# Split weights at rotating columns: nine weight buffers made 64 bytes longer, each block begun 0 to 15 columns in

## The chip, the cores and the metric

The kernel runs on one core of a Trainium2 chip. The metric is the device time of one execution in microseconds; it is compared with the time of the kernel before on the same chip.

## The reference

Two transformer-like blocks follow each other on 512 tokens of width 1024, all in fp32. Most of the work is in products of activations with weights:

```python
def squared_relu_mlp(h, w1, w2):
    return jnp.square(jax.nn.relu(h @ w1)) @ w2
...
    for i in range(DEPTH):
...
        x = x + rms_norm(m, g[1])
        h = rms_norm(x, g[2])
        x = x + rms_norm(squared_relu_mlp(h, mlp_w1[i], mlp_w2[i]), g[3])
...
    ffn = (jax.nn.silu(n2 @ w_gate) * (n2 @ w_up)) @ w_down
    return h + ffn
```

`DEPTH` is 2: in the first of its rounds `m` comes from a short convolution beside a latent attention, in the second from a convolution of 31 taps between two products. The last lines are of the second block, which has attention with a forget gate and 16 extra tokens, and pooling, ahead of them. The MLP width is 4096 in the first block, 2816 in the second.

## The kernel before

Activations lie transposed: channels in the 128 partitions, the 512 tokens along the free dimension. So an activation tile is 128 x 512, and a product is a sum over tiles of 128 channels, accumulated in one PSUM buffer `ps`.

Precision comes from splitting. Each fp32 number is kept as a high part, rounded to the format fp32r by a copy, and a low part, the difference. A tile of activations `P` is `[128, 2, 512]`: high parts in the first 512 columns, low parts in the next. Weights are split in the same way into buffers `W`, `[128, 2, 512]`. `mm3` then makes three matmuls for each product (lines 357 to 359): high weights by high activations, high weights by low activations, low weights by high activations. The weights are the stationary operand (128 columns, loaded by a weight load of their own ahead of every matmul), the activations are the moving one, 512 columns at a time or 256 where a stage works in halves.

All weights stand in one array in the order in which they are used. `make_plan` writes that order down as pieces of 128 columns (some have 256, those of the forget gate 8), and `pack` puts pieces into blocks of up to 512 columns, and two blocks into one load. There are 578 blocks. The class `Weights` runs through them: `dma` brings a load of two blocks into one of three `raw` buffers on SyncE's queue, and `advance` splits a block into one of nine `W` buffers: the high part on ScalarE (line 284), the low part on VectorE (line 286), or on GpSimd for 55 blocks of the convolution module. In the program's order a block is split four blocks before it is used (`AHEAD`); in time ScalarE runs ahead as far as the nine buffers allow. A call of `W(name, k, t)` gives the high and the low columns of a piece: columns `c` to `c + n` of its block.

In the built program every `W` buffer has 4096 bytes in each partition and so has every `P` buffer; the first `W` buffer begins 163,072 bytes behind the first `P` buffer, which is 637 times 256.

Four other places matter below:

- `run_pe` (line 1112) makes part of the 31-tap convolution with matmuls: the stationary operand is a tap matrix of `W`, the moving one 256 columns of a tile `x` that begin at column `s`, 0 to 15 in turn. High parts of `x` lie in columns 0 to 271, low parts in 272 to 543. It makes 384 matmuls.
- `forget_gate` (line 1333) uses eight pieces of 8 columns, by 512 moving columns. They stand in one block behind three pieces of 128 columns, at columns 384, 392 and so on to 440. Each is used for three matmuls.
- `conv_dve` (line 1068) makes the other half of the convolution on VectorE: tap `t` reads 512 columns of a tile from column `t` on, 0 to 30 (line 1082). The tile is written from column 15 on (line 1139).
- `conv_pe` (line 1099) writes its tile `x` on ScalarE from columns 8 and 7 on (line 1109).

Of the kernel before, what the change touches and what calls it, by code (L numbers as in the profile page):

```python
# [12 lines left out]
F32R = mybir.dt.float32r  # L13
# [8 lines left out]
T = 512  # L22
# [222 lines left out]
class Weights:  # L245
# [30 lines left out]
    def advance(self, b):  # L276
        nc = self.nc
        while self.nsplit <= min(b + self.AHEAD, len(self.blocks) - 1):
            load, start, cols = self.blocks[self.nsplit]
            while self.ndma <= min(load + self.RAW - 1, len(self.loads) - 1):  # L280
                self.dma()
            w = self.w_pool.tile([128, 2, T], F32R, name="W")
            r = self.raw[load][:, start:start + cols]
            nc.scalar.activation(out=w[:, 0, :cols], in_=r, func=AF.Copy)  # L284
            eng = nc.gpsimd if self.nsplit in self.on_pool else nc.vector
            eng.tensor_sub(out=w[:, 1, :cols], in0=r, in1=w[:, 0, :cols].bitcast(F32))  # L286
            self.w[self.nsplit] = w
            self.nsplit += 1
# [1452 lines left out]
```

## Time and profile before

| | |
|---|---|
| median of 2 runs | 1764.86 us (1763.05 to 1766.67) |
| profiled execution | 1765.45 us |
| its span, first to last instruction | 1763.7 us |
| TensorE busy | 1723.2 us, 98% |
| VectorE busy | 1091.3 us, 62% |
| ScalarE busy | 802.3 us, 45% |
| GpSimd busy | 272.2 us, 15% |
| matmuls | 8828 |
| DMA | 167.26 MB, mean 95 GB/s |

The times of instructions come from one profiled execution. PE is TensorE's matmul, PEld its weight load, which overlaps matmuls, DVE is VectorE, ACT is ScalarE, POOL is GpSimd. A matmul's shown duration reaches from its start to a modelled end and is longer than the distance to the next start, so distances are read from starts.

### The profile page before, as it was taken

What the parts mean: (1) busy time and instruction counts of PE and PEld (TensorE: products, weight loads), DVE (VectorE), ACT (ScalarE), POOL (GpSimd) and SP (SyncE); (2) the same over time, 40 slices, a digit from 0 to 9 for tenths busy, and PEclk for the clock granted to TensorE, in tenths of its full rate; (3) what the DMA queues carried; (4) which work ended last, traced back from release to release, by engine and by line L of the source; (5) the groups of instructions that cost most, each with busy time, mean ns of one, the idle gap of its engine ahead of it and who ended that gap; (6) DMA issues with size and microseconds to landing.
All of it is one profiled execution on the core that took longest, in us unless ns stands there. A gap on an engine that the chain in (4) does not pass through costs nothing.

```text
span 1763.7 us, 23141 instructions
## 1 busy us (share of the span) xinstructions
PE 1723.2 (98%) x8828; PEld 1459.7 (83%) x8828; DVE 1091.3 (62%) x1771; ACT 802.3 (45%) x1461; POOL 272.2 (15%) x339
## 2 busy tenths in 40 slices
PE   9999999999999999999999999989999999999999
PEld 7778888888888878999888888888687888888887
DVE  6988786344444789958544444487897555344452
ACT  6546655333333445675543333357665443232331
POOL 3413330000000355503000000041223200000000
PEclk9999999999999999999999999999999999999999
DMA  5231313223322132512322222222223323222221
GB/s 196 73 106 55 108 49 120 96 98 101 100 96 96 49 108 96 180 60 73 118 99 96 96 96 96 96 96 69 78 62 98 98 98 101 97 96 96 96 96 60
DMA packets 49887, 167.26 MB, mean 95 GB/s; under 512 B 6848, under 2 KB 7296, under 8 KB 49776
## 3 DMA queue, kind: packets, MB, share of 16 engines
q1 hardware_dynamic: 47776, 160.70, 27.8%
q0 software_dynamic: 1936, 5.07, 1.0%
q8 instruction: 69, 1.13, 0.3%
q14 instruction: 42, 0.34, 0.1%
q10 hardware_dynamic: 64, 0.02, 0.0%
HBM read 158.25 MB, written 4.19 MB: 92 GB/s over the span
## 4 chain that ended last, share of the span: by engine, by line
PE 80%; DVE 11%; issue 3%; ACT 2%; POOL 2%; DMA 1%; SPq 0%; POOLq 0%; DVEq 0%; ACTq 0%
PE ps L358 26%; PE ps L357 26%; PE ps L359 26%; DVE P L968 1%; DVE W L286 1%; PE ps L623 1%; DVE P L401 1%; POOL P L971 1%; DVE S L1477 1%; DVE S L424 1%; DVE P L398 1%; DMA raw<-in_w 1%; ACT S L450 1%; DVE S L422 1%; DVE S L420 0%
## 5 line engine op out<-in xcount | busy, mean ns | idle before, releaser
L357 PE MATMUL ps<-P,W 128*128 128x512 f32 (+1 forms) x2541 | 928.2, 365 | 5.9 <-DVE S L1130 2.8
L358 PE MATMUL ps<-P,W 128*128 128x512 f32 (+1 forms) x2541 | 924.8, 364 | 5.8 <-DVE P L401 5.8
L359 PE MATMUL ps<-P,W 128*128 128x512 f32 (+1 forms) x2541 | 923.4, 364 | 0.0
L284 ACT ACTIVATE W<-raw 128x512 fp32r<-128x512 f32 x578 | 357.1, 629 | 651.4 <-PE ps L359 609.0
L286 DVE TENSOR_TENSOR W<-raw,W 128x512 fp32r<-128x512 f32 x523 | 371.4, 717 | 382.2 <-ACT W L284 379.6
L357 PEld LDWEIGHTS ps<-P,W 128*128 128x128 f32 x2541 | 482.2, 190 | 83.3 <-DVE S L1130 3.2
L358 PEld LDWEIGHTS ps<-P,W 128*128 128x128 f32 x2541 | 482.9, 190 | 81.0 <-DVE P L401 6.9
L359 PEld LDWEIGHTS ps<-P,W 128*128 128x128 f32 x2541 | 482.3, 190 | 75.3 <-DVE W L286 0.4
L971 POOL TENSOR_TENSOR P<-P 128x256 f32<-128x256 f32 x48 | 45.5, 956 | 773.3 <-DVE P L968 772.2
L398 DVE TENSOR_TENSOR P<-S,P 128x512 fp32r<-128x512 f32 (+3 forms) x134 | 93.8, 706 | 50.4 <-ACT P L397 49.8
L397 ACT ACTIVATE P<-S 128x512 fp32r<-128x512 f32 (+3 forms) x134 | 81.5, 614 | 63.8 <-DVE S L1664 25.9
L286 POOL TENSOR_TENSOR W<-raw,W 128x512 fp32r<-128x512 f32 x55 | 73.0, 1352 | 37.7 <-ACT W L284 33.7
L1082 DVE SCALAR_TENSOR_TENSOR ps<-P,vec,ps 128x512 f32<-128x512 f32 x116 | 77.8, 745 | 0.0
L400 ACT ACTIVATE P<-P,vec 128x256 fp32r<-128x256 f32 (+1 forms) x80 | 43.7, 549 | 50.4 <-POOL P L971 30.1
L1029 DVE SCALAR_TENSOR_TENSOR S<-ps,S 128x512 f32<-128x512 f32 x64 | 43.6, 689 | 34.1 <-PE ps L359 34.1
L401 DVE SCALAR_TENSOR_TENSOR P<-P,vec 128x256 fp32r<-128x256 f32 (+1 forms) x80 | 54.2, 691 | 9.7 <-ACT P L400 9.5
L470 POOL TENSOR_TENSOR S<-S 128x256 f32<-128x256 f32 (+1 forms) x45 | 48.1, 1069 | 76.6 <-ACT S L469 74.3
L469 ACT ACTIVATE S<-P 128x256 f32<-128x256 f32 (+1 forms) x105 | 46.4, 473 | 17.8 <-DVE P L1056 11.9
L636 POOL TENSOR_TENSOR P<-S,P 128x512 fp32r<-128x512 f32 (+1 forms) x24 | 34.3, 1428 | 112.3 <-DVE P L635 95.7
L1049 DVE TENSOR_TENSOR P<-ps,P 128x512 f32<-128x512 f32 x42 | 29.0, 691 | 28.7 <-PE ps L359 28.7
L623 PE MATMUL ps<-P 128*128 128x512 f32 (+3 forms) x160 | 41.2, 375 | 2.2 <-DVE S L1443 0.9
L470 DVE TENSOR_TENSOR S<-S 128x256 f32<-128x256 f32 (+1 forms) x60 | 33.1, 551 | 14.4 <-ACT S L469 13.4
(263 smaller groups left out, 1300.7 us busy)
## 6 DMA issues: line engine op xcount, KB each, us to landing
raw<-in_w SPq DMA_DIRECT2D x286, 512.0 KB
P<-in_xT SPq DMA_DIRECT2D x8, 256.0 KB
P<-in_xT POOLq DMA_DIRECT2D x8, 256.0 KB, 5.4
keep<-P SPq DMA_DIRECT2D x8, 256.0 KB
P<-P SPq DMA_DIRECT2D x16, 128.0 KB
P<-keep POOLq DMA_DIRECT2D x8, 256.0 KB, 5.4
out<-P SPq DMA_DIRECT2D x7, 256.0 KB
raw<-in_w SPq DMA_DIRECT2D x2, 256.0 KB
```

The source lines that it names most:

```text
L284: nc.scalar.activation(out=w[:, 0, :cols], in_=r, func=AF.Copy)
L286: eng.tensor_sub(out=w[:, 1, :cols], in0=r, in1=w[:, 0, :cols].bitcast(F32))
L357: mm(ps, w[0], x[0], start=first, stop=False)
L358: mm(ps, w[0], x[1], start=False, stop=False)
L359: mm(ps, w[1], x[0], start=False, stop=last)
L397: nc.scalar.activation(out=hi, in_=src, func=AF.Copy)
L398: nc.vector.tensor_sub(out=lo, in0=src, in1=hi.bitcast(F32))
L401: nc.vector.scalar_tensor_tensor(out=lo, in0=src, scalar=scale, in1=hi.bitcast(F32), op0=OP.mult, op1=OP.subtract)
L470: (eng or nc.vector).tensor_add(out=acc, in0=acc, in1=t)
L623: mm(o[:m], k, q[:, pl, c0:], start=n == 0 and m == 128, stop=n == len(keys) - 1 and mask is None)
L971: ins = eng.tensor_add(out=x[k][:, cols], in0=x[k][:, cols], in1=m[k][:, cols]).ins
L1082: V.scalar_tensor_tensor(out=dst if dst is not None and t == taps[-1] else acc, in0=u, scalar=w, in1=acc, op0=OP.mult, op1=OP.add)
```

## The change

Each `W` buffer gets 16 columns more (64 bytes in each partition). Block number `n` uses the 1024 columns that begin at column `n % 16` of its buffer, and views them as `[128, 2, 512]` again, so all reads and writes of the block go through the shifted view. `raw`, `P` and all other buffers stay where they are.

```diff
-            w = self.w_pool.tile([128, 2, T], F32R, name="W")
+
+            o = self.nsplit % 16
+            w = self.w_pool.tile([128, 2 * T + 16], F32R, name="W")[:, o:o + 2 * T].rearrange("p (l t) -> p l t", l=2)
             r = self.raw[load][:, start:start + cols]
             nc.scalar.activation(out=w[:, 0, :cols], in_=r, func=AF.Copy)
             eng = nc.gpsimd if self.nsplit in self.on_pool else nc.vector
```

The sequence of instructions on each engine, and what each waits for, is the same in both programs.

## Rows read from the trace of the kernel before

**Rows 1.** the page's first part: busy time of each engine

```profile
span 1763.7 us, 23141 instructions
...
PE 1723.2 (98%) x8828; PEld 1459.7 (83%) x8828; DVE 1091.3 (62%) x1771; ACT 802.3 (45%) x1461; POOL 272.2 (15%) x339
```

**Rows 2.** windows: busy by engine (instructions), granted clock, DMA share, GB/s

```profile
1000.00:1100.00 100.00, 100.00 (x443) 82.83 (x442) 45.57 (x66) 34.94 (x57) 0.00 (x0) 1.00 0.31 100
...
1200.00:1300.00 100.00, 94.26 (x639) 76.22 (x636) 88.77 (x186) 65.78 (x143) 17.66 (x17) 1.00 0.20 57
...
641.50:644.50 3.00, 3.00 (x8) 2.32 (x7) 3.00 (x6) 1.58 (x3) 0.01 (x1) 0.50 0.42 158
```

**Rows 3.** waits: engine, line <- releaser: us in total, times, longest

```profile
ACT W L284 <- PE ps L359: 609.0, 344, 2.9
...
DVE W L286 <- ACT W L284: 379.6, 304, 3.8
...
PEld ps L357 <- ACT W L284: 0.8, 1, 0.8
...
PEld ps L359 <- DVE W L286: 0.4, 1, 0.4
```

**Rows 4.** groups by shape, whole span: count, busy us, mean ns, idle before

```profile
L357 PE MATMUL ps<-P,W 128*128 128x512 f32 x1879 | 735.0, 391 | 4.0 <-DVE S L1130 2.8 <-ACT P L400 1.2
...
L357 PE MATMUL ps<-P,W 128*128 128x256 f32 x654 | 190.0, 291 | 1.9 <-ACT P L397 0.8 <-ACT P L400 0.6 <-DVE P L1689 0.5
...
L357 PEld LDWEIGHTS ps<-P,W 128*128 128x128 f32 x2533 | 481.5, 190 | 82.2 <-DVE S L1130 3.2 <-ACT P L400 2.4 <-ACT P L397 1.4
...
L284 ACT ACTIVATE W<-raw 128x512 fp32r<-128x512 f32 x576 | 356.2, 629 | 651.4 <-PE ps L359 609.0 <-DMA raw<-in_w 22.8 <-PE ps L1264 5.4
...
L286 DVE TENSOR_TENSOR W<-raw,W 128x512 fp32r<-128x512 f32 x521 | 370.3, 718 | 382.2 <-ACT W L284 379.6
```

**Rows 5.** timeline of TensorE at half clock: start us, us, instruction

```profile
641.95 0.63 PE L358 MATMUL ps<-P,W 128*128 128x512 f32 x1
...
644.08 0.63 PE L357 MATMUL ps<-P,W 128*128 128x512 f32 x1
```

**Rows 6.** timeline of TensorE, forget gate

```profile
1196.86 0.39 PE L357 MATMUL ps<-P,W 128*8 128x512 f32 x1
...
1197.54 0.40 PE L357 MATMUL ps<-P,W 128*8 128x512 f32 x1
...
1202.39 0.18 PE L357 MATMUL ps<-hm,W 128*8 128x32 f32 x1
```

**Rows 7.** timeline of TensorE, convolution's first matmul and the one after its last

```profile
696.10 0.28 PE L357 MATMUL ps<-P,W 128*128 128x256 f32 x1
...
741.38 0.38 PE L1177 MATMUL ps<-P,onesf 128*128 128x256 f32 x1
```

**Rows 8.** groups of TensorE in that convolution (one of three equal ones)

```profile
L358 PE MATMUL ps<-P,W 128*128 128x256 f32 x128 | 35.9, 280 | 0.0
```

**Rows 9.** timeline of TensorE, a run of 256-column matmuls after it

```profile
765.45 0.28 PE L357 MATMUL ps<-P,W 128*128 128x256 f32 x1
...
781.29 0.40 PE L357 MATMUL ps<-P,W 128*128 128x512 f32 x1
```

**Rows 10.** groups of TensorE in that run (one of three equal ones)

```profile
L358 PE MATMUL ps<-P,W 128*128 128x256 f32 x44 | 12.5, 283 | 0.0
```

**Rows 11.** weight loads of 64 and 32 columns: ns min/median/max

```profile
L1264 PEld LDWEIGHTS ps<-W,hm x80: 133/134/223, 1181.9 to 1331.8; 128*64 128x64 f32 x80
...
L1263 PEld LDWEIGHTS ps<-W,hm x70: 107/108/113, 1184.7 to 1331.7; 128*32 128x32 f32 x70
```

**Rows 12.** single lines with shifted columns: ns min/median/max

```profile
L1082 DVE SCALAR_TENSOR_TENSOR ps<-P,vec,ps x116: 736/744/753, 647.1 to 738.2; 128x512 f32<-128x512 f32 x116
...
L1109 ACT ACTIVATE P<-P x16: 657/661/682, 673.3 to 705.7; 64x512 fp32r<-64x512 f32 x16
...
L1139 DVE SCALAR_TENSOR_TENSOR P<-S,vec x4: 734/882/1292, 641.0 to 660.1; 128x512 f32<-128x512 f32 x4
```

## The prediction

> **What bounds the kernel now.** I read the page's busy times first, then equal stretches of the span, then who waits for whom, then the groups of instructions by shape, and last the starts of single matmuls. TensorE is busy 1723.2 of 1763.7 us [rows 1]. In a plain stretch of the MLP, 1000 to 1100 us, it is busy for all 100 us, while VectorE is busy 45.57 and ScalarE 34.94 [rows 2]. The waits say the same from the other side: the ScalarE half of the weight split stands 609.0 us waiting for a matmul to free a W buffer, and the VectorE half 379.6 us for the ScalarE half, but weight loads of lines 357 and 359 waited for a split only 0.8 and 0.4 us in the whole run [rows 3]. So the split runs ahead as far as nine buffers let it, and what sets the end is how long one matmul takes after another.
>
> I call that distance from start to start the pitch. TensorE's matmuls by weights of W are 3 x 1879 with 512 moving columns and 3 x 654 with 256, 7599 in all [rows 4]. [...] At the full clock one takes 226.7 ns ((1197.54 - 1196.86) / 3 in [rows 6]). [...]
>
> **What the change takes away, adds and moves.** No instruction is added, removed or put elsewhere on any engine, and no wait is: the sequence of all five engines is the one of before. Only addresses change. W buffers step by 4160 bytes instead of 4096, and a block begins 0 to 60 bytes behind its buffer's start. Today the stationary columns of a full block, and the moving columns of P in a plain matmul, begin at addresses that differ by a multiple of 256 bytes; afterwards the difference takes all values of four bytes in turn (9 buffers and 16 columns come round every 144 blocks, and there are 578).
>
> Edits with a price of nothing: the 36 KB of W grow by 576 bytes and push nothing else. No DMA writes W; raw keeps its place, so landings stay.
>
> Writes and reads of the split. ScalarE writes high parts, VectorE reads them back and writes low parts, all at shifted columns. The nearest rows: VectorE's convolution taps read P at 0 to 30 columns' shift, and 116 of them lie between 736 and 753 ns; ScalarE's writes that begin at columns 7 and 8 lie between 657 and 682; one VectorE write into P from column 15 on takes 734 at least, so the odd start has no visible price [rows 12]. By the whole spread of these rows the split would cost 17 ns x 521 = 8.9 us more of VectorE and 25 ns x 576 = 14.4 us more of ScalarE. Neither reaches TensorE: a block of 512 columns feeds 12 matmuls, 2.7 us, and costs 0.63 us of ScalarE and 0.72 of VectorE [rows 4], with nine buffers of lead. That cover would be gone where VectorE is 88.77% busy (1200 to 1300 us, [rows 2]) if its part doubled; nothing in the rows is near that. I take 0, between 0 and 2 us.
>
> Weight loads. A load of 128 columns takes 190 ns [rows 4] and begins with the matmul ahead of it, so at a pitch of 226.7 there are 37 ns of cover. At 256 columns the pitch is 120.0 ns (15.84 us over 132 matmuls, [rows 9, 10]), and loads follow each other at that pitch, so they overlap or are cut close; a longer load would show there first. From loads of 64 and 32 columns, 134 and 108 ns [rows 11], a column costs 26 / 32 = 0.8 ns, so four columns cost 3.3 ns.
>
> The pitch itself. The trace has no 128-column load from a shifted place, so I bound it by the two nearest rows. (a) The convolution on TensorE has the moving operand at 0 to 15 columns' shift and W unshifted: 384 matmuls of 256 columns in 45.28 us, 117.9 ns each [rows 7, 8], 2.1 below the 120.0 of unshifted ones. If it is the difference of the two addresses that counts, every other matmul gets this: -2.1 x (7599 - 384) = -15.2 us. (b) The forget gate has weights of 8 columns that begin at column 384 for the first k and at 392 to 440 for the other seven. The first three matmuls have a pitch of 226.7, the next 21 take 4.85 us, 231.0 each [rows 6]: +4.3 x 7599 = +32.7 us. These have the shift on the right operand but 8 columns only, and other causes may be in them. Between -15.2 and +32.7 I take 0: the two nearest rows have opposite signs, the first shifts the operand that this change leaves alone, and the weights are loaded well ahead of their use, so that their place should show less than the moving operand's.
>
> [...]
>
> **Sum.** 0 of TensorE, 0 of the split. The profiled execution took 1765.45 us, 1.75 more than its span; the median of the runs, 1764.86, is 0.6 lower, and I put the forecast on it: **1765 us**. A measurement of this kernel tells about 2% (35 us) from no change.
>
> **The rivals.**
> First, the difference of addresses counts, and an even spread over all of them is better than the one of today: -15.2 us, 1750. For it speaks that the pitch of the convolution differs with nothing but the column. Against it: the forget gate, and that a moving stream, not a load, was shifted there. [...]
> Second, slower: a stationary operand that does not lie in step with the moving one costs its matmul the 4.3 ns of the forget gate, at every matmul of lines 357 to 359: 1765 + 32.7 = 1798. It decides from the first shifted block on, and would show in the MLP as a pitch of 231. For it: these are the only shifted weights in the trace, and the step comes exactly with the shift. Against it: (a), and that the seven shifts, 32 to 224 bytes, all cost alike, which an address rule would hardly do.
> [...]
>
> **How the numbers follow.** Forecast (pitch within 0.8 ns of now, 1759 to 1771): 0.50. First rival, about 1743 to 1759: 0.20, and a gain beyond it 0.05. Third rival, 1771 to 1790: 0.11. Second rival, 1790 to 1806: 0.14. The range 1743 to 1800 leaves out the larger gain, some of the first rival's lower edge, and the upper half of the second: together 0.15 to 0.2. Faster by over 2% (below 1730) is the 0.05; slower by over 2% (above 1800) is the upper half of the second rival with a little for a split that comes late, 0.10; within 2% is the rest, 0.85.
>
> **What would show it.** Right: 442 or 443 matmuls in 100 us of the MLP as now [rows 2], the group of line 286 on VectorE within 20 ns of 718, waits for W still under 2 us. First rival: 447 per 100 us and a 256-column pitch of 118. Second: 434 or 435 per 100 us. [...] Wrong altogether would be the forecast if the pitch goes block by block with the column, by more than 2 ns in the mean, or if weight loads begin to wait for line 286.

## Result and profile after

| | before | after |
|---|---|---|
| median of 2 runs | 1764.86 us | 1791.92 us (1791.58 to 1792.27) |
| ratio, 95% interval | | 1.0153 [1.0108, 1.0199] |
| span of the profiled execution | 1763.7 us | 1789.8 us |
| TensorE busy | 1723.2 us | 1748.9 us |

The kernel became 27 us slower, 1.5%: within the stated range, clear of noise, and far from the 1765 us of the forecast. Two lines were added, so lines 284, 286 and 357 to 359 of before are 286, 288 and 359 to 361 here.

The page's first part after the change, to be laid beside [rows 1]:

```profile
span 1789.8 us, 23141 instructions
...
PE 1748.9 (98%) x8828; PEld 1455.9 (81%) x8828; DVE 1091.1 (61%) x1771; ACT 803.4 (45%) x1461; POOL 267.4 (15%) x339
```

TensorE's busy time grew by 25.7 us and the span by 26.1; VectorE and ScalarE are where they were, to 1.1 us. So the time went into matmuls. The stretch of the MLP in the view of windows (columns as in [rows 2]):

```profile
1000.00:1100.00 100.00, 100.00 (x431) 80.73 (x430) 43.55 (x63) 33.16 (x54) 0.00 (x0) 1.00 0.29 95
```

The clock is the full one, TensorE is never idle, and 431 matmuls stand where 443 stood [rows 2]. The groups by shape, which answer to [rows 4], tell which matmuls:

```profile
L359 PE MATMUL ps<-P,W 128*128 128x512 f32 x1879 | 745.8, 397 | 3.0 <-DVE S L1132 2.2 <-ACT P L402 0.6 <-ACT W L286 0.2
...
L360 PEld LDWEIGHTS ps<-P,W 128*128 128x128 f32 x2533 | 479.9, 189 | 89.1 <-DVE P L403 6.8
...
L288 DVE TENSOR_TENSOR W<-raw,W 128x512 fp32r<-128x512 f32 x521 | 370.6, 719 | 397.4 <-ACT W L286 393.8
L286 ACT ACTIVATE W<-raw 128x512 fp32r<-128x512 f32 x576 | 357.5, 630 | 678.2 <-PE ps L361 603.5 <-DVE P L1051 34.5 <-DMA raw<-in_w 10.1
L359 PE MATMUL ps<-P,W 128*128 128x256 f32 x654 | 187.7, 288 | 2.7 <-ACT P L402 1.4 <-ACT P L399 0.8 <-DVE P L1691 0.5
```

A matmul of 512 columns went from a mean of 391 to 397 ns, one of 256 from 291 to 288. The first matmuls of the products grew by 745.8 - 735.0 = 10.8 us at 512 columns and fell by 190.0 - 187.7 = 2.3 at 256. Three matmuls to a product make 3 x (10.8 - 2.3) = 25.5 us, which is the whole change. Not all of the 3 ns at 256 columns are the pitch: the means have matmuls at the half clock in them (before, those from 605.24 to 606.95 us show 0.41 us in place of 0.28, in a stretch whose granted clock was 0.50), and the mean granted clock of the two executions differs a little (0.991 before, 0.993 after). In the run of 132 matmuls that [rows 9, 10] show, the pitch went from 120.0 to (791.07 - 775.43) / 132 = 118.5 ns:

```profile
775.43 0.28 PE L359 MATMUL ps<-P,W 128*128 128x256 f32 x1
...
791.07 0.40 PE L359 MATMUL ps<-P,W 128*128 128x512 f32 x1
```

The weight load keeps its 189 to 190 ns, and the split costs what it did: 719 against 718 on VectorE, 630 against 629 on ScalarE. The waits of weight loads for a split stay at nothing, as in [rows 3]:

```profile
PEld ps L359 <- ACT W L286: 0.9, 1, 0.9
...
PEld ps L361 <- DVE W L288: 0.2, 1, 0.2
```

### The profile page after: what moved, and what is told of

It is laid out like the page before. It is cut to its first block, busy times and chain, and to the rows that moved or that the text cites. A ratio compares the mean times of both kernels' runs of the same rounds, so it can differ in the third digit from the quotient of the medians.

```text
span 1789.8 us, 23141 instructions
## 1 busy us (share of the span) xinstructions
PE 1748.9 (98%) x8828; PEld 1455.9 (81%) x8828; DVE 1091.1 (61%) x1771; ACT 803.4 (45%) x1461; POOL 267.4 (15%) x339
## 4 chain that ended last, share of the span: by engine, by line
PE 82%; DVE 11%; issue 3%; ACT 3%; POOL 1%; DMA 0%; SPq 0%; POOLq 0%; DVEq 0%; ACTq 0%
PE ps L359 26%; PE ps L360 26%; PE ps L361 26%; PE ps L625 1%; DVE P L970 1%; DVE W L288 1%; DVE P L400 1%; DVE P L403 1%; DVE S L1479 1%; POOL P L973 1%; ACT S L452 1%; DVE S L426 1%; DVE S L424 1%; DVE S L422 0%; DVE P L1525 0%
## 5 line engine op out<-in xcount | busy, mean ns | idle before, releaser
L288 POOL TENSOR_TENSOR W<-raw,W 128x512 fp32r<-128x512 f32 x55 | 67.1, 1243 | 42.1 <-ACT W L286 37.9
L1051 DVE TENSOR_TENSOR P<-ps,P 128x512 f32<-128x512 f32 x42 | 29.0, 692 | 30.7 <-PE ps L361 30.7
```

## Experiments

Three theories stood at the start. A: a matmul's pitch depends on the difference between the address of the weights and that of the activations, modulo 256 bytes, and 0 is a good place for 512 columns. B: what counts is where the weights lie by themselves (how far into its buffer a block begins, or, as B2, their absolute address). C: the shifted writes and reads of the split cost. Times are compared with the kernel before on the same chip, whose median was 1762 to 1764 us each time. "Difference" is always weights less activations, modulo 256 bytes.

**e1: only the longer buffers, no rotation.**

```diff
-            o = self.nsplit % 16
+            o = 0
```

> The buffers keep their 64 bytes more, but every block begins at column 0, so that the difference of the addresses of weights and activations is 0, 64, 128 or 192 modulo 256: 0 for three buffers of nine. Theory A (the pitch of 512-column matmuls depends on the difference of the two addresses, and 0 modulo 256 is its best place): six of nine buffers pay some 5 ns per matmul, 5 x 5637 x 6/9 = 19 us, so about 1784 us and 437 or 438 matmuls in 100 us of the MLP. [...] Theory C (the split's writes and reads at odd columns cost, on ScalarE and VectorE): 1765 us.

Measured: 1779.53 against 1762.39 us, ratio 1.0094 [1.0072, 1.0117]. The window of the MLP:

```profile
1000.00:1100.00 100.00, 100.00 (x436) 1.00 0.27 95
```

436 matmuls against 443, with every block at column 0. So neither the place of a block in its buffer nor C is what costs these 17 us (19 were expected). The timeline shows the cost buffer by buffer. A block feeds twelve matmuls; the rows are the starts of three blocks in a row, and of the one behind them:

```profile
1021.56 0.39 PE L359 MATMUL ps<-P,W 128*128 128x512 f32 x1
...
1024.28 0.39 PE L359 MATMUL ps<-P,W 128*128 128x512 f32 x1
...
1027.03 0.40 PE L359 MATMUL ps<-P,W 128*128 128x512 f32 x1
...
1029.82 0.39 PE L359 MATMUL ps<-P,W 128*128 128x512 f32 x1
```

They take 2.72, 2.75 and 2.79 us, or 226.7, 229 and 232.5 ns for each matmul. The nine blocks from 1004.96 to 1029.82 us, one for each buffer, take 2.80, 2.80, 2.80, 2.73, 2.75, 2.72, 2.72, 2.75 and 2.79 us: three at the old pitch, two at 229 and four at 232.5 to 233. Nine buffers that step by 64 bytes have three differences of 0 and two each of 64, 128 and 192, and e5 below has these three pitches for them (226.7 ns at 0, 229.2 at 192, 232.5 to 233.1 at 128 and 64).

**e2, e3, e4: activations and weights moved by 64 bytes, together or one alone**, all in the kernel before. e2 adds a tile of 16 columns ahead of everything; e3 adds it and takes as much from the unused tile `pad` that lies between S and raw; e4 enlarges `pad` alone.

```diff
+        gap = cp.tile([128, 16], F32, name="gap")                        # e2, e3
+        nc.vector.memset(gap[:, 0:1], 0.0)                               # e2, e3
...
-            nc.vector.memset(pad.tile([128, 32], F32, name="pad")[:, 0:1], 0.0)
+            nc.vector.memset(pad.tile([128, 16], F32, name="pad")[:, 0:1], 0.0)   # e3; 48 in e4
```

> The kernel before with P, S, raw and W all moved by 64 bytes: no difference of addresses changes, all absolute addresses do. Theory A: 1765 us, pitch 226.7 ns. Theory B2 (the absolute place of the weights counts, whatever the activations do): a pitch like that of the changed kernel, 230 to 233 ns, and 1783 to 1795 us. Theory C: 1765 us.

> The kernel before with P moved by 64 bytes and W and raw left where they are (difference 192 modulo 256). Theory A: pitch at 512 columns 229 to 233 ns, at 256 columns 118, so 1765 + 3 to 6 ns x 5637 - 2 ns x 1960 = 1778 to 1795 us. Theory B2 (the weights' own address counts): 1765 us. Theory C: 1765 us.

> The kernel before with W and raw moved by 64 bytes and P left where it is (difference 64 modulo 256, the same for all blocks). Theory A: pitch at 512 columns about 233 ns, 1765 + 6 x 5637 ns - 2 ns x 1960 = 1795 us. Theory B2: slower too. Theory C: 1765 us. Apart from e3, this tells whether the sign of the difference matters.

Measured: e2 (difference 0) 1761.93 us, ratio 1.0002 [0.9987, 1.0017]; e3 (192) 1775.28 us, 1.0074 [1.0050, 1.0097]; e4 (64) 1793.07 us, 1.0172 [1.0142, 1.0201]. The same window of e2, of e3, then of e4:

```profile
1000.00:1100.00 100.00, 100.00 (x443) 1.00 0.27 95
```

```profile
1000.00:1100.00 100.00, 100.00 (x439) 1.00 0.28 98
```

```profile
1000.00:1100.00 100.00, 100.00 (x430) 1.00 0.27 95
```

Moving both costs nothing, moving either does, and in e3 the weights have not moved at all. So it is the difference; B2 falls, and the size depends on which difference it is: 64 costs well over twice what 192 does (30.7 against 12.9 us, the second just under the 13 to 30 expected). e4 also points to the other sign at 256 columns, 286 ns for the first matmul of a product where [rows 4] has 291 (these means depend on the granted clock too, which was 0.995 in the mean here and 0.991 there; e5 has the size):

```profile
L357 PE MATMUL ps<-P,W 128*128 128x256 f32 x654 | 186.6, 286 | 2.3 <-ACT P L400 0.9 <-ACT P L397 0.8 <-DVE P L1689 0.5
```

**e5: matmuls alone.** A kernel of its own, with constant tiles; the rest of the computation is left out. Its core:

```python
def run(p, w, cols, n=128, reps=4):
    ps = psp.tile([128, T], F32, name="ps")
    for r in range(reps):
        for c in range(4):
            wc = slice(128 * c, 128 * c + n)
            for a, b in ((0, 0), (0, 1), (1, 0)):
                mm(ps[:n, :cols], w[:, a, wc], p[:, b, :cols], ...)
```

> It leaves out the whole computation: matmuls of constant tiles alone, with no other engine at work, 48 for each place: weights shifted by 0 to 256 bytes against activations, activations shifted by 4 to 128 bytes, both shifted by 64 or 128, at 512 and 256 columns. Theory A (TensorE's own two reads meet, by the difference of their addresses modulo 256): the pitches of the kernels come back without any other engine: at 512 columns 226.7 ns for 0 and 256, 233 for 64 and 128, 229 for 192, at 256 columns 120, 114 to 115, 118 and 115 to 117; both shifted by 64 gives 226.7 and 120; weights shifted by 32 bytes with 8 columns give about 231. Theory D (the difference matters only because ScalarE, VectorE or DMAs read and write the same buffers at the same time): all pitches alike. The stretch in which shifted and unshifted weights alternate tells whose shift a start waits for: the weights that are loaded beside a stream, or those that the stream uses.

From 40 to 408 us of the trace nothing but TensorE is at work. The timeline of TensorE (start, time, instruction, count): `P64b` is an activation tile begun 64 bytes in, `W4b` a weight tile begun 4 bytes in, and 1/48 of the distance between two starts is the pitch of the first of them.

```profile
34.24 11.05 PE L46 MATMUL ps<-P0b,W0b 128*128 128x512 f32 x48
45.12 11.32 PE L46 MATMUL ps<-P0b,W4b 128*128 128x512 f32 x48
56.28 11.23 PE L46 MATMUL ps<-P0b,W8b 128*128 128x512 f32 x48
67.35 11.36 PE L46 MATMUL ps<-P0b,W16b 128*128 128x512 f32 x48
78.55 11.35 PE L46 MATMUL ps<-P0b,W32b 128*128 128x512 f32 x48
89.74 11.36 PE L46 MATMUL ps<-P0b,W48b 128*128 128x512 f32 x48
100.94 11.36 PE L46 MATMUL ps<-P0b,W64b 128*128 128x512 f32 x48
112.13 11.40 PE L46 MATMUL ps<-P0b,W96b 128*128 128x512 f32 x48
123.37 11.32 PE L46 MATMUL ps<-P0b,W128b 128*128 128x512 f32 x48
134.53 11.37 PE L46 MATMUL ps<-P0b,W160b 128*128 128x512 f32 x48
145.73 11.16 PE L46 MATMUL ps<-P0b,W192b 128*128 128x512 f32 x48
156.73 11.36 PE L46 MATMUL ps<-P0b,W224b 128*128 128x512 f32 x48
167.92 11.04 PE L46 MATMUL ps<-P0b,W256b 128*128 128x512 f32 x48
178.80 5.91 PE L46 MATMUL ps<-P0b,W0b 128*128 128x256 f32 x48
184.55 5.84 PE L46 MATMUL ps<-P0b,W4b 128*128 128x256 f32 x48
...
212.79 5.61 PE L46 MATMUL ps<-P0b,W64b 128*128 128x256 f32 x48
218.24 5.92 PE L46 MATMUL ps<-P0b,W96b 128*128 128x256 f32 x48
224.00 5.85 PE L46 MATMUL ps<-P0b,W128b 128*128 128x256 f32 x48
...
252.51 11.60 PE L46 MATMUL ps<-P4b,W0b 128*128 128x512 f32 x48
263.94 11.28 PE L46 MATMUL ps<-P16b,W0b 128*128 128x512 f32 x48
275.06 11.16 PE L46 MATMUL ps<-P64b,W0b 128*128 128x512 f32 x48
286.05 11.32 PE L46 MATMUL ps<-P128b,W0b 128*128 128x512 f32 x48
297.21 11.08 PE L46 MATMUL ps<-P64b,W64b 128*128 128x512 f32 x48
308.13 11.09 PE L46 MATMUL ps<-P128b,W128b 128*128 128x512 f32 x48
319.06 6.07 PE L46 MATMUL ps<-P4b,W0b 128*128 128x256 f32 x48
324.96 5.77 PE L46 MATMUL ps<-P16b,W0b 128*128 128x256 f32 x48
...
353.41 11.05 PE L46 MATMUL ps<-P0b,W0b 128*8 128x512 f32 x48
364.30 11.26 PE L46 MATMUL ps<-P0b,W32b 128*8 128x512 f32 x48
375.39 11.26 PE L46 MATMUL ps<-P0b,W64b 128*8 128x512 f32 x48
```

At 512 columns the pitch is (45.12 - 34.24) / 48 = 226.7 ns for a difference of 0 and again for 256 (10.88 / 48). It is 232.5 at 4 bytes, 230.6 at 8, 233.3 at 16, 233.1 at 64, 232.5 at 128, 229.2 at 192. Shifting the activations by 64 costs what its difference of 192 costs, (286.05 - 275.06) / 48 = 229.0, and shifting both by 64 gives back 227.5. At 256 columns 0 has 119.8 and 64 has 113.5, but the gain is not there at every difference: 96 has 120.0, as much as 0. Activations shifted by 4 bytes, a difference of 252, cost at both widths, 238.1 ns at 512 and 122.9 at 256. That 113.5 lies just under the 114 to 115 expected, and 192 has 117.7 for 115 to 117. At 512 columns these are the numbers of the kernels, without any other engine at work: theory A holds, and a clash with the reads and writes of other engines is not the cause. The 8-column weights of the forget gate come back too: 226.9 unshifted, 231.0 at 32 bytes, as in [rows 6]. Each place was measured once, in one execution. In the stretch that alternates weights at 0 and at 64 the pitch lies half way (230) and does not tell whose shift a start waits for.

**e6, e7: the rotation alone, and its measure.** To keep buffers apart by a multiple of 256 bytes they need 4352 bytes each, and only eight fit.

```diff
-NP, NS, NW = 32, 9, 9
+NP, NS, NW = 32, 9, 8
...
-            w = self.w_pool.tile([128, 2 * T + 16], F32R, name="W")[:, o:o + 2 * T].rearrange("p (l t) -> p l t", l=2)
+            w = self.w_pool.tile([128, 2 * T + 64], F32R, name="W")[:, o:o + 2 * T].rearrange("p (l t) -> p l t", l=2)
```

e6 keeps `o = self.nsplit % 16`, e7 has `o = 0`.

> Eight W buffers of 2T + 64 columns (4352 bytes, a multiple of 256) with the rotation by 0 to 15 columns: the other part of the change alone, differences 0 to 60 modulo 256. Theory A: from the changed kernel's blocks with a difference of 4 to 60 bytes, pitch about 232 ns, so 1762 + 5 x 5637 ns - 2 x 1960 ns = 1786 us. [...] It is to be compared with the next one, which has eight buffers and no rotation.

> Eight W buffers of 4352 bytes, every block at column 0: all differences 0 modulo 256. Theory A: pitch 226.7 ns, 1762 us as before (one buffer less costs nothing, since the split is some 20 us ahead). If buffers set the pace somewhere, slower.

Measured: e6 1808.0 us, 1.0252 [1.0234, 1.0269]; e7 1782.03 us, 1.0095 [1.0079, 1.0112]. Against its measure the rotation costs 26.0 us, against the 24 expected; both absolute forecasts missed, because losing the ninth buffer was not free. e7's pitch is the old one, 443 matmuls in the MLP's window (e6 has 432). Its span is 16.5 us longer than before: 10.6 us of it is TensorE's busy time, the other 5.9 is idle time, in part in waits for a split. The longer busy time goes with a lower mean clock, which by an estimate from the two clocks and spans is worth 0.013 x 1780 - 0.009 x 1764 = 7 us. Below are the page's first part and the views of waits and of clocks; before: 0.8 us of waits in [rows 3], and a mean clock of 0.991.

```profile
PE 1733.8 (97%) x8828; PEld 1465.8 (82%) x8828; DVE 1094.8 (61%) x1771; ACT 804.8 (45%) x1461; POOL 271.6 (15%) x339
```

```profile
PEld ps L359 <- ACT W L286: 4.0, 6, 0.9
```

```profile
core 0: 1780.2 us, clock 0.987
```

The rest of what the missing buffer cost was not taken apart.

**e8: a difference of 64 where only 256 columns are read.** As e7, with

```diff
+HALF = {*range(55, 68), *range(183, 196), *range(253, 260), *range(263, 276), *range(391, 404), 577}
...
+            o = 16 if self.nsplit in HALF else 0
```

> As the one before, but the blocks that are read by matmuls of 256 columns (all but those of the convolution) begin 16 columns in, a difference of 64. Theory A: those 1578 matmuls go from 119.8 to about 115 ns, 4.8 x 1578 = 7.6 us less, about 1755 us, and nothing changes at 512 columns. If the sign at 256 columns was an accident of the blocks in the other kernels: 1762 us.

Measured: 1778.83 us, 3.2 less than e7 (ratios 1.0081 [1.0066, 1.0096] and 1.0095 [1.0079, 1.0112]): the sign expected, half the size, and the intervals overlap. Part of the missing half seems to be the clock: four of e8's six executions had a mean clock of 0.983 or 0.984, where e7's four had 0.986 or 0.987. The two at 0.987 took 1773.72 and 1774.20 us, against 1777.02 to 1782.14 for e7's three at the same clock. That is nearer to the 7.6 us expected, though from few executions.

**e9 to e12: the same with nine buffers**, the room taken from S, the pool of scratch tiles (`NS = 8`).

> Nine W buffers again, of 4352 bytes, every block at column 0, so all differences are 0 modulo 256; the room comes from one S buffer less (eight for nine). It is the measure for the next one. Theory A: pitches of the kernel before, 226.8 and 119.8 ns; the time is that of before plus what the missing S buffer costs, 1763 to 1775 us.

> As the one before, with the blocks that only 256-column matmuls read (all but the convolution's) begun 16 columns in, a difference of 64. Theory A: 115 to 116 ns for those 1578 matmuls, 4 x 1578 = 6 us less than the one without; it beats the kernel before only if the missing S buffer costs less than that. If a difference of 64 did not help at 256 columns: the time of the one without.

Measured: 1793.97 us (1.0177 [1.0162, 1.0193]) and 1793.38 us (1.0178 [1.0162, 1.0194]). Both expectations were built on a wrong address: the missing S buffer of 2176 bytes had moved W by 128 modulo 256. By accident it is one more point for A: a difference of 128 for all blocks in e9, and in e10 of 192 for those that begin 16 columns in. With `pad` at 64 columns the difference is 0 again:

> e9 with 128 bytes more ahead of raw and W. In e9 the missing S buffer of 2176 bytes had moved raw and W by 128 modulo 256, so that its differences were 128 and not 0 as its expectation said; here they are 0. Theory A: pitch 226.8 and 119.8 ns, 1763 us and what the missing S buffer costs. If the 1794 us of e9 were the price of the S buffer, 1794 us again.

> e10 with the same 128 bytes: the difference is 0 for blocks that 512-column matmuls read and 64 for those that only 256-column matmuls read. Theory A: 115 to 116 ns at 256 columns, 226.8 at 512, 4 x 1578 = 6 us less than the one before; 1756 to 1760 us if the S buffer costs nothing.

Measured: e11 1767.28 us, 1.0026 [1.0014, 1.0039]: 26.7 us came back with 128 bytes of padding and nothing else. e12 1766.57 us, 1.0016 [1.0005, 1.0027]: 0.7 us under e11, not the 6 expected, and above the kernel before. The page's first part and two of the longest waits of TensorE, of e11 and then of e12:

```profile
PE 1725.2 (98%) x8828; PEld 1460.2 (83%) x8828; DVE 1096.4 (62%) x1771; ACT 802.5 (45%) x1461; POOL 270.9 (15%) x339
...
PE ps L361 <- DVE P L404: 6.0, 5, 2.2
...
PE ps L963 <- ACT P L400: 3.0, 4, 1.6
```

```profile
PE 1719.8 (97%) x8828; PEld 1453.1 (82%) x8828; DVE 1098.6 (62%) x1771; ACT 802.7 (45%) x1461; POOL 270.5 (15%) x339
...
PE ps L361 <- DVE P L404: 6.7, 5, 3.3
...
PE ps L963 <- ACT P L400: 4.7, 4, 1.8
```

TensorE is busy 5.4 us less, as the pitch says: the run of 132 matmuls of 256 columns goes from 120.4 ns (starts at 765.65 and 781.54 us in e11) to 116.4 (768.72 and 784.08 in e12). But the spans are 1766.3 and 1766.7 us, so TensorE's idle time grew by 5.8 us. Waits for splits of activations (lines 361 and 963 above) account for 2.4 of it; where the rest arose, and whether it is the same in other executions, is not shown. No kernel here beats the one before.

## Why the prediction was right and wrong

The bound was read rightly: the pitch of matmuls sets the time, the split has cover, its shifted writes and reads cost nothing (719 against 718 ns, 630 against 629), no wait was added. The change of the span is the change of TensorE's busy time to 0.4 us.

The forecast of 1765 us, no change, was wrong. That 1791.92 still lies in the stated range is due to the second rival, which had been given 1790 to 1806 us and a chance of 0.14, and not to the reasoning for the forecast. What was to show it "wrong altogether" came about: the pitch goes with where a block begins (e1, e5), and the window's 431 matmuls for 443 mean over 6 ns more each.

The step that failed is the last of the cost, "Between -15.2 and +32.7 I take 0". Its two ends were not bounds of one number. Row (a) was of 256 moving columns and row (b) of 512, and the effect can have opposite signs at the two widths: e5 gives +6.4 ns at 512 and -6.3 at 256 for the same difference of 64. Each row had to be applied to its own matmuls: +4.3 x 5637 - 2.1 x (1962 - 384) = 24.2 - 3.3 = +20.9 us, 1786, instead of being averaged into nothing. So the second rival was the right mechanism with a price somewhat low at 512 columns (4.3 against about 6 ns) and wrongly carried to 256 columns; its 1798 came nearest of all the cases. The first rival's sign is right at 256 columns only. In place of the 0 the runs showed some +6 ns at 512 columns (10.8 us over 1879 matmuls) and, in the run of 132 matmuls, -1.5 at 256; TensorE's busy time grew by 25.7 us.

Three reasons that were given against the second rival fell. "The first shifts the operand that this change leaves alone": e2 and e3 show that either operand's shift does it, since only the difference counts. "The weights are loaded well ahead of their use, so that their place should show less than the moving operand's": it shows as much, 5.8 ns for weights shifted by 128 bytes and 5.8 for activations shifted by 128. It shows with loads of 8 columns too, though less (4.1 ns against 6.4 at 32 bytes), so it is not the long load alone that makes it. The seven shifts, it said, "all cost alike, which an address rule would hardly do": in e5 the shifted weights cost 4 to 7.5 ns at 512 columns at every difference but 0, 256 and 192 (2.5), so nearly alike is what the rule looks like; the place before the change is the exception. Why the forget gate's piece at 192 bytes, with 8 columns, paid as much as its neighbours is not shown.

For the third rival (1771 to 1790 us) no run shows a term: the mean weight load stayed at 189 to 190 ns, and at 512 columns weights shifted by 4 bytes cost 5.8 ns of pitch and by 16 bytes 6.6 (e5). For a gain beyond the first rival's no run shows a term either: at 512 columns no shift in e5 had a pitch below the 226.7 ns of a difference of 0, and at 256 the lowest was 113.5 for 119.8. The pitch at a difference of 0 is 226.7 ns with other engines at work [rows 6] and without them (e5); where TensorE's own two operands lie to each other matters, by up to 7.5 ns of 226.7 with the weights shifted (96 bytes) and 11.4 with the activations (4 bytes).

Why a difference of 0 suits 512 columns and not 256, and what in the chip makes the difference matter, stays open: no run here looks inside the pitch.

## What to carry to other kernels

Where matmuls follow each other without a gap, the pitch, read from starts, is a quantity to look at by itself: at 512 fp32r columns it grew by 2 to 3% when the weights were shifted by 4 to 128 bytes against the activations (from 226.7 to between 230.6 and 234.2 ns in e5). At that width keep the two apart by a multiple of 256 bytes (226.7 ns at 0 and at 256 in e5), and look at the addresses again whenever a buffer ahead of them changes its size: one buffer of 2176 bytes less cost 32 us, and 128 bytes of padding put 27 of them back. At another width, measure first. When two rows of the trace price the same thing with opposite signs, ask first in what else they differ (here the width) and apply each to its own share.

## What was not expected of the hardware

The sign can turn with the width: a difference of 64 bytes costs 6.4 ns of 226.7 at 512 columns and saves 6.3 of 119.8 at 256. The last of nine weight buffers is worth 18 us (1782.03 against 1763.92), though the split seemed some 20 us ahead (an estimate: eight blocks of 2.72 us), and more of that stands in TensorE's busy time (10.6 us of the profiled execution's 16.5, at a mean clock of 0.987 for 0.991) than in its idle time (5.9). And a saving of 5.4 us of TensorE's busy time at 256 columns was worth nothing measurable, because its idle time grew by as much (5.8 us, e12 against e11).
